# One emission order for the streams of two token mixers

## The chip, the core and the metric

The kernel runs on one core of a Trainium2 chip. The time is device microseconds of one execution. TensorE (PE) multiplies matrices, VectorE (DVE), ScalarE (ACT) and GpSimd (POOL) work element by element, and SyncE (SP) issues nearly all loads. Each of these takes its own instructions in the order in which the built program lists them, and waits on semaphores for the others.

## What is computed

One decoder layer on 256 tokens of width 1,024, in float32: a SwiGLU layer, then two token mixers side by side, then cross-attention to a memory, then a second SwiGLU layer, each with a residual and a layer norm. The change is in the mixers:

```python
g_ssd, g_att, z, xbc, dt_raw, q, c_kv, q_idx, k_idx, w_idx = split_cols(x @ w_in, IN_SPLITS)
y_ssd = ssd_branch(z, xbc, dt_raw, ...)
y_att = dsa_branch(q, c_kv, q_idx, k_idx, w_idx, ...)
merged = sigmoid(g_ssd) * (y_ssd @ w_proj_ssd) + sigmoid(g_att) * (y_att @ w_proj_att)
x = layer_norm(ALPHA * x + merged @ w_out)
```

`ssd_branch` is a state-space mixer: a causal convolution of width 4 over 2,048 channels and a SiLU, then a scan in two chunks of 128 tokens over 16 heads, a gate by `z` and a norm by groups. `dsa_branch` is sparse attention: 16 index heads give each query a score for each key, the 64 best keys stay (top-k), and 16 heads attend to them. The projection of `y_ssd` needs the whole scan. The attention's softmax needs the top-k. The gates `g_ssd` and `g_att` need neither.

## The kernel before

**Weights.** A unit of work is a matrix of 1,024 by 256 weights in two pieces of 512 KB. A piece is loaded by SP into one of 4 `raw` buffers, ACT rounds it into `whi` (line 150), DVE takes the rest into `wlo` (line 151), with 6 buffers each. PE then runs 24 matmuls of 256 columns (line 116): high by high, high by low, low by high for eight blocks of 128 features. A unit asks for a PSUM buffer of the group `mm`, of which there are 4; scores take one of 2 in `s`, transposes and small products one of 2 in `t`. Where a call passes `pool=True`, POOL takes the rest of the second piece instead of DVE.

**Streams.** The mixers are written as generators, and `fly` interleaves them. It keeps a clock of its own, `self.pe`, which counts matmul columns, and each generator yields either a pause on that clock or the name of a mark that it waits for. Of the streams that are due it always resumes the first in the list. What `fly` emits is then scheduled once more by the tile framework, which may set instructions of one engine ahead of others. The order that results is fixed in the program.

**Two groups.** The first `fly` runs `ssd_decay` (softplus and decay, lines 533 to 565), `latent` (the keys' latent, `cT`), `xbc` (the convolution: 8 units, and after each the convolution of its 2 blocks of 128 channels on ACT and DVE, lines 454 to 458) and `k_index`. The second runs `dsa` (index projections `w_qidx`, the scores with sums `acc` on DVE in line 695, the top-k in lines 701 and 702, then `w_q` and the attention heads), `ssd` (the scan: `E` are the decays, `xdt` the scaled inputs, `xtok` the output by token, `yT` the normed output turned for the projection) and `fill_mixers` (keys and values of the first four heads, gate 0 in 4 units of `w_gate`, then, after the mark "yT", 4 units of `w_pssd`, then gate 1). Gate 0 waits for the mark "zs", and the second piece of each of its units goes to POOL. Its buffer is slot 4, which holds `zs` (the gate by `z`) before.

**What runs when.** In the program that results, PE does the 16 pieces of `w_xbc` in a row, then the 8 of `w_qidx` between index scores and the scan, then `w_q`, gate 0, and from there one attention head for about every unit of `w_q`, `w_pssd` and gate 1. The last two pieces of gate 1 stand behind the last head, and `w_patt` follows.

Of the kernel before, what the change touches and what calls it, by code (L numbers as in the profile page):

```python
# [19 lines left out]
F32 = mybir.dt.float32  # L20
# [5 lines left out]
P = 128  # L26
T = 256
# [17 lines left out]
WARM = 4  # L45
HEAD_US = 2.4
TOPK_US = 12.0
SSD_US = (2.0, 6.0, 1.0, 5.0)


class Layer:
# [381 lines left out]
    def xbc(self, xT, xtok, bc):  # L433

        nc, t = self.nc, self.t
        late = []

        def flush(n):
            for b, v in (late.pop(0) for _ in range(min(n, len(late)))):
                tp = self.psum("t")[:, :T].rearrange("p (b c) -> p b c", c=P)  # L440
                for tb in range(NTB):
                    self.transpose(tp[:, tb, :], v[:, tb * P:(tb + 1) * P])
                nc.scalar.copy(xtok[:, :, b * P:(b + 1) * P], tp)
        for u in (4, 5, 6, 7, 0, 1, 2, 3):
            ps = self.psum("mm")
            for _ in self.a_steps(ps, t["w_xbc"][u], xT, u % 2 == 1):
                flush(max(0, len(late) - 2))
                yield 0.0
            for i in range(2):
                b = 2 * u + i  # L450
                src = ps[:, i * T:(i + 1) * T]
                v = self.small([P, T], "wa", bufs=4) if b < 8 else bc[:, b - 8, :]
                cw = self.conv_w[:, b, :]
                nc.scalar.activation(v, src, AF.Identity, bias=self.conv_b[:, b:b + 1], scale=cw[:, 3:4])
                for d in (1, 2, 3):
                    self.last_conv = nc.vector.scalar_tensor_tensor(  # L456
                        v[:, d:], src[:, :T - d], cw[:, 3 - d:4 - d], v[:, d:], op0=ALU.mult, op1=ALU.add)
                self.last_silu = nc.scalar.activation(v, v, AF.Silu)
                if b < 8:
                    late.append((b, v))  # L460
            yield 0.0
        yield "kidx"
        flush(len(late))

    def small_proj(self, xT):

# [17 lines left out]
    def latent(self, cT):  # L484

        nc = self.nc
        for tb, c in enumerate(self.ctok):
            sq = self.small([P, 256], "wa", bufs=4)
            ss = self.small([P, 1], "css", bufs=2)
            nc.scalar.activation(sq, c, AF.Square, accum_out=ss)  # L490
            nc.vector.tensor_scalar_mul(ss, ss, 1.0 / 256.0)
            rs = self.rstd(ss, 1, RMS_EPS)
            nc.vector.tensor_scalar_mul(c, c, rs)
        yield 8.0
        for tb, c in enumerate(self.ctok):
            tp = self.psum("t")[:, :256].rearrange("p (k c) -> p k c", c=P)
            for k in range(2):
                self.transpose(tp[:, k, :], c[:, k * P:(k + 1) * P])
                h, l, w = cT[0][:, k, tb * P:(tb + 1) * P], cT[1][:, k, tb * P:(tb + 1) * P], self.kv_w[:, k:k + 1]
                nc.scalar.activation(h, tp[:, k, :], AF.Copy, scale=w)  # L500
                nc.vector.scalar_tensor_tensor(l, tp[:, k, :], w, h.bitcast(F32), op0=ALU.mult, op1=ALU.subtract)
            yield 3.0

    def k_index(self, kidx):

# [28 lines left out]
    def ssd_decay(self):  # L534
# [24 lines left out]
        for tb in range(NTB):  # L559
            nc.gpsimd.dma_start(scr[tb].rearrange("(h l) -> h l", l=P), csT[:, tb, :])  # L560
            e = self.big((7, 9)[tb], F32, (P, H, P), "E")
            nc.gpsimd.dma_start(e.rearrange("p h l -> p (h l)"), scr[tb].partition_broadcast(P))
            nc.gpsimd.tensor_tensor(e, e, cs[:, tb, :].unsqueeze(2).to_broadcast([P, H, P]), op=ALU.subtract)
            self.E.append(e)

    def ssd(self, zs, xtok, bc, yT):

        nc = self.nc
        cs, E, dt, dskip = self.cs, self.E, self.dtr, self.hv[:, 2 * H:3 * H]
        xdt = self.big(3, F32, (P, NTB, D), "xdt")  # L570
        sx = self.big(8, F32, (P, 2, D), "S0xe")
# [81 lines left out]
    def dsa(self, xT, kidx, cT, oT):  # L653
# [5 lines left out]
        def project(name, u, scale):  # L659

            ps = self.psum("mm")
            yield from self.a_steps(ps, t[name][u], xT)
            v = ps.rearrange("p (a b) -> p a b", b=T)
            q = [self.small([P, 2, T], tag, F32R, bufs) for tag, bufs in (("w2a", 2), ("w2e", 4))]
            for i in range(2):
                a, b = slice(i * HD, (i + 1) * HD), slice((1 - i) * HD, (2 - i) * HD)
                nc.scalar.mul(q[i][a], v[a], scale)
                nc.vector.scalar_tensor_tensor(q[i][b], v[a], scale, q[i][a].bitcast(F32),
                                               op0=ALU.mult, op1=ALU.subtract)
            qs.append(q)  # L670

        def scores(q, hh, kh, kl):
# [6 lines left out]
                self.mm(o, q[:, hh // 2, ts], kl, False, True)  # L679
            return ps[:, :384]  # L680
        qs = []
        yield from project("w_qidx", 0, 1.0)
        for u in range(4):
            if u < 3:
# [89 lines left out]
    def keys_values(self, u, cT):  # L774
# [1 line left out]

        nc = self.nc
        w, = self.weight(self.t["w_ukv"][u])
        s = self.big((11, 6)[u % 2], F32R, name="kv")
        kh = s[:, :1024].rearrange("p (i a b) -> p i a b", i=2, b=T)  # L780
        kl = s[:, 1024:].rearrange("p (i a b) -> p i a b", i=2, b=T)
        v0 = self.small([P, 2, T], "w2c", F32R, 2)
# [19 lines left out]
        self.kv.append((kh, kl, vh, vl, v1))  # L802
        yield 0.0

    def fill_mixers(self, xT, cT, yT, gates):
        nc, t = self.nc, self.t
        yield from self.keys_values(0, cT)
        self.done.add("vk")

        def gate(i, u):  # L810
            ps = self.psum("mm")
            yield from self.a_steps(ps, t["w_gate"][4 * i + u], xT, i == 0)
            nc.scalar.activation(gates[i][:, 2 * u:2 * u + 2, :], ps.rearrange("p (a b) -> p a b", b=T),
                                 AF.Tanh, scale=0.5)
        yield "zs"
        for u in range(4):
            yield from gate(0, u)
        yield "yT"
        for u in range(4):
            ps = self.psum("mm")  # L820
            yield from self.a_steps(ps, t["w_pssd"][u], yT)
            g = gates[0][:, 2 * u:2 * u + 2, :]
            nc.vector.scalar_tensor_tensor(g, g, 1.0, ps.rearrange("p (a b) -> p a b", b=T),
                                           op0=ALU.add, op1=ALU.mult)
        for u in range(4):
            yield from gate(1, u)


    def mem_v(self, memT):
# [87 lines left out]
    def run(self):  # L917
# [35 lines left out]
        kidx = [self.small([P, T], tag, F32R, 1) for tag in ("kidxh", "kidxl")]  # L953
        xtok = self.big(10, F32, (P, NTB, D), "xtok")
        bc = self.big(5, F32, (P, 8, T), "bcT")
        self.fly(self.ssd_decay(), self.latent(cT), self.xbc(xT, xtok, bc), self.k_index(kidx))
        yT = self.pairT(7, 9, "yT")
        oT = self.pairT(3, 10, "oT")
        gates = [self.big((4, 5)[i], F32, (P, KB, T), "gate") for i in range(2)]
        self.fly(self.dsa(xT, kidx, cT, oT), self.ssd(zs, xtok, bc, yT), self.fill_mixers(xT, cT, yT, gates))  # L960
        mT = self.pairT(6, 8, "mT")
        for u in range(4):
            ps = self.a_unit(t["w_patt"][u], oT).rearrange("p (a b) -> p a b", b=T)
            k = slice(2 * u, 2 * u + 2)
# [113 lines left out]
```

## Time and profile before

| | us |
|---|---|
| median of 3 runs | 814.89 |
| lowest, highest | 809.25, 816.68 |
| profiled execution | 814.78 |
| its span | 812.9 |
| PE busy | 789.4 |
| DVE busy | 592.4 |
| ACT busy | 448.4 |
| POOL busy | 68.2 |

The span is the time from the first to the last instruction of one profiled execution. PE's busy time counts a matmul from its start to a modelled end, and neighbours overlap by more than half, so work on PE is better counted by the distance from one start to the next. The granted clock of PE is given in shares of full speed.

### The profile page before, as it was taken

The numbers are of one execution on the slowest core, as the hardware profiler recorded it, in microseconds if no ns is written. First come the engines' busy times: TensorE is split into PE (matmuls) and PEld (weight loads), VectorE is DVE, ScalarE is ACT, GpSimd is POOL, SyncE is SP. The second block draws the span as 40 slices with busy tenths as digits, with TensorE's granted clock in tenths as the row PEclk, the third lists the DMA queues.
The fourth block names the chain that finished last, engine by engine and source line by source line (L and its number), as shares of the span: only waits on it lengthen the run. The fifth ranks groups of instructions, "written<-read, shape, count | busy, mean of one in ns | idle before, by whom it ended". The sixth has DMA issues, their size and how long they took to land.

```text
span 812.9 us, 13145 instructions
## 1 busy us (share of the span) xinstructions
PE 789.4 (97%) x5070; PEld 717.5 (88%) x5070; DVE 592.4 (73%) x960; ACT 448.4 (55%) x782; POOL 68.2 (8%) x69
## 2 busy tenths in 40 slices
PE   8999999999989998989999999999999999999996
PEld 5888888887889997989999998899988988888885
DVE  4868776448588989698889767965659777776445
ACT  5756565433476684477667644544444666565330
POOL 1100000000032451230000000200002000000000
PEclk9999999999999999799999999999999999999999
DMA  7876555553656621236444456574433755555531
GB/s 249 271 267 224 193 182 194 187 200 104 210 189 228 208 74 51 81 108 233 165 150 135 158 175 215 170 276 161 156 120 134 256 191 195 192 184 194 192 105 53
DMA packets 39919, 142.90 MB, mean 176 GB/s; under 512 B 4592, under 2 KB 4896, under 8 KB 39472
## 3 DMA queue, kind: packets, MB, share of 16 engines
q1 hardware_dynamic: 38016, 134.63, 49.4%
q0 software_dynamic: 1840, 7.43, 2.9%
q8 instruction: 40, 0.66, 0.3%
q14 instruction: 23, 0.19, 0.1%
HBM read 140.97 MB, written 1.06 MB: 175 GB/s over the span
## 4 chain that ended last, share of the span: by engine, by line
PE 74%; DVE 11%; issue 8%; ACT 4%; DMA 2%; POOL 1%; SPq 0%; DVEq 0%; ACTq 0%; POOLq 0%
PE ps_mm L116 69%; DVE wlo L151 3%; PE ps_t L116 2%; PE ps_t L120 2%; DMA raw<-in_ffn_in_dram 2%; ACT whi L150 1%; PE ps_s L116 1%; DVE acc L695 1%; DVE acc L702 1%; DVE wa L456 1%; DVE m L701 1%; DMA raw<-in_w_pssd_dram 0%; POOL rstd L289 0%; DVE kv L794 0%; DVE kv L793 0%
## 5 line engine op out<-in xcount | busy, mean ns | idle before, releaser
L151 DVE TENSOR_TENSOR wlo<-raw,whi 128x1024 fp32r<-128x1024 f32 (+2 forms) x245 | 301.0, 1231 | 129.1 <-ACT whi L150 125.1
L150 ACT CAST whi<-raw 128x1024 fp32r<-128x1024 f32 (+2 forms) x253 | 263.2, 1044 | 188.1 <-PE ps_mm L116 124.6
L116 PE MATMUL ps_mm<-x1T,whi 128*128 128x256 f32 x768 | 143.9, 288 | 0.0
L116 PE MATMUL ps_mm<-x0T,whi 128*128 128x512 f32 x352 | 123.7, 400 | 2.9 <-ACT whi L150 2.1
L116 PEld LDWEIGHTS ps_mm<-x1T,whi 128*128 128x128 f32 x768 | 122.3, 195 | 0.0
L116 PE MATMUL ps_mm<-x1T,wlo 128*128 128x256 f32 x384 | 110.2, 287 | 0.0
L116 PE MATMUL ps_mm<-x3T,whi 128*128 128x512 f32 x304 | 105.6, 392 | 0.0
L116 PE MATMUL ps_mm<-x0T,wlo 128*128 128x256 f32 x352 | 97.0, 282 | 0.3 <-DVE wlo L151 0.3
L116 PE MATMUL ps_mm<-x3T,wlo 128*128 128x256 f32 x304 | 85.1, 280 | 0.0
L116 PEld LDWEIGHTS ps_mm<-x0T,whi 128*128 128x128 f32 x352 | 65.8, 188 | 20.6 <-ACT whi L150 3.6
L116 PEld LDWEIGHTS ps_mm<-x1T,wlo 128*128 128x128 f32 x384 | 75.1, 195 | 0.0
L116 PEld LDWEIGHTS ps_mm<-x3T,whi 128*128 128x128 f32 x304 | 56.9, 187 | 12.4
L116 PEld LDWEIGHTS ps_mm<-x0T,wlo 128*128 128x128 f32 x352 | 65.7, 189 | 1.6 <-DVE wlo L151 1.4
L116 PE MATMUL ps_mm<-whi,ah 128*128 128x512 f32 x154 | 60.2, 391 | 0.0
L116 PE MATMUL ps_mm<-wlo,ah 128*128 128x512 f32 x154 | 60.1, 390 | 0.0
L116 PE MATMUL ps_mm<-whi,al 128*128 128x512 f32 x154 | 59.9, 389 | 0.0
L116 PEld LDWEIGHTS ps_mm<-x3T,wlo 128*128 128x128 f32 x304 | 57.5, 189 | 0.0
L289 POOL TENSOR_TENSOR rstd<-rstd,mhalf 128x1 f32<-128x1 f32 (+1 forms) x12 | 11.3, 941 | 537.0 <-DVE rstd L288 537.0
L177 DVE TENSOR_TENSOR wa<-wa,ps_mm 128x256 f32<-128x256 f32 x82 | 34.0, 418 | 30.2 <-ACT wa L176 30.1
L347 ACT ACTIVATE wa<-wa 128x256 f32<-128x256 f32 x41 | 17.1, 417 | 48.1 <-DVE wa L177 48.1
L116 PEld LDWEIGHTS ps_mm<-whi,al 128*128 128x128 f32 x154 | 28.9, 188 | 6.2
L116 PEld LDWEIGHTS ps_mm<-whi,ah 128*128 128x128 f32 x154 | 29.0, 188 | 5.6
(296 smaller groups left out, 1551.5 us busy)
## 6 DMA issues: line engine op xcount, KB each, us to landing
raw<-in_ffn_in_dram SPq DMA_DIRECT2D x87, 512.0 KB, 4.1
raw<-in_ffn_out_dram SPq DMA_DIRECT2D x44, 512.0 KB, 3.5
raw<-in_w_xbc_dram SPq DMA_DIRECT2D x16, 512.0 KB, 4.3
raw<-in_w_gate_dram SPq DMA_DIRECT2D x16, 512.0 KB, 3.4
raw<-in_w_z_dram SPq DMA_DIRECT2D x8, 512.0 KB, 3.6
raw<-in_w_qidx_dram SPq DMA_DIRECT2D x8, 512.0 KB, 3.9
raw<-in_w_q_dram SPq DMA_DIRECT2D x8, 512.0 KB, 3.5
raw<-in_w_pssd_dram SPq DMA_DIRECT2D x8, 512.0 KB, 4.6
```

Source lines behind the costliest of these rows:

```text
L116: self.nc.tensor.matmul(out, a, b, start=start, stop=stop)
L120: self.nc.tensor.transpose(out, in_, self.ident)
L150: self.nc.scalar.copy(hi, src)
L151: (engine or self.nc.vector).tensor_sub(lo, src, hi.bitcast(F32))
L177: self.nc.vector.tensor_add(out, out, ps[:, :T])
L289: self.nc.gpsimd.tensor_tensor(v, v, self.mhalf[:, :n], op=ALU.pow)
L347: nc.scalar.activation(sg, self.join(gate, sg), AF.Silu)
L456: self.last_conv = nc.vector.scalar_tensor_tensor(v[:, d:], src[:, :T - d], cw[:, 3 - d:4 - d], v[:, d:], op0=ALU.mult, op1=ALU.add)
L695: nc.vector.scalar_tensor_tensor(acc[:, s], rl[:, s], self.widx[:, tb, h:h + 1], prev[:, s], op0=ALU.mult, op1=ALU.add)
L701: nc.vector.max(m8, acc[:, s])
L702: nc.vector.match_replace(out=acc[:, s], in_to_replace=m8, in_values=acc[:, s], imm_value=KILL)
```

## The change

All seven streams go into one `fly`. `xbc` now yields a pause of 4.0 after each unit, in which streams behind it in the list are resumed: the index projections and scores, the first keys and values, and gate 0. Marks take the place of the group's end: `ssd` waits for "E" (decays broadcast) and "xtok" (the convolution emitted whole), `fill_mixers` for "cT", `dsa` for "kidx". Gate 0 no longer waits for "zs" and no longer uses POOL, and its buffer is slot 6; odd units of keys and values, and then `mT`, take slot 4. `gate` becomes a method.

```diff
--- before.py
+++ after.py
@@ -45,6 +45,7 @@
 WARM = 4
 HEAD_US = 2.4
 TOPK_US = 12.0
+XBC_US = 4.0
 SSD_US = (2.0, 6.0, 1.0, 5.0)
 
 
@@ -458,9 +459,9 @@
                 self.last_silu = nc.scalar.activation(v, v, AF.Silu)
                 if b < 8:
                     late.append((b, v))
-            yield 0.0
-        yield "kidx"
+            yield XBC_US
         flush(len(late))
+        self.done.add("xtok")
 
     def small_proj(self, xT):
 
@@ -500,6 +501,7 @@
                 nc.scalar.activation(h, tp[:, k, :], AF.Copy, scale=w)
                 nc.vector.scalar_tensor_tensor(l, tp[:, k, :], w, h.bitcast(F32), op0=ALU.mult, op1=ALU.subtract)
             yield 3.0
+        self.done.add("cT")
 
     def k_index(self, kidx):
 
@@ -562,10 +564,13 @@
             nc.gpsimd.dma_start(e.rearrange("p h l -> p (h l)"), scr[tb].partition_broadcast(P))
             nc.gpsimd.tensor_tensor(e, e, cs[:, tb, :].unsqueeze(2).to_broadcast([P, H, P]), op=ALU.subtract)
             self.E.append(e)
+        self.done.add("E")
 
     def ssd(self, zs, xtok, bc, yT):
 
         nc = self.nc
+        yield "E"
+        yield "xtok"
         cs, E, dt, dskip = self.cs, self.E, self.dtr, self.hv[:, 2 * H:3 * H]
         xdt = self.big(3, F32, (P, NTB, D), "xdt")
         sx = self.big(8, F32, (P, 2, D), "S0xe")
@@ -679,6 +684,7 @@
                 self.mm(o, q[:, hh // 2, ts], kl, False, True)
             return ps[:, :384]
         qs = []
+        yield "kidx"
         yield from project("w_qidx", 0, 1.0)
         for u in range(4):
             if u < 3:
@@ -776,7 +782,7 @@
 
         nc = self.nc
         w, = self.weight(self.t["w_ukv"][u])
-        s = self.big((11, 6)[u % 2], F32R, name="kv")
+        s = self.big((11, 4)[u % 2], F32R, name="kv")
         kh = s[:, :1024].rearrange("p (i a b) -> p i a b", i=2, b=T)
         kl = s[:, 1024:].rearrange("p (i a b) -> p i a b", i=2, b=T)
         v0 = self.small([P, 2, T], "w2c", F32R, 2)
@@ -802,28 +808,28 @@
         self.kv.append((kh, kl, vh, vl, v1))
         yield 0.0
 
+    def gate(self, g, i, u, xT):
+
+        ps = self.psum("mm")
+        yield from self.a_steps(ps, self.t["w_gate"][4 * i + u], xT)
+        self.nc.scalar.activation(g[:, 2 * u:2 * u + 2, :], ps.rearrange("p (a b) -> p a b", b=T), AF.Tanh, scale=0.5)
+
     def fill_mixers(self, xT, cT, yT, gates):
-        nc, t = self.nc, self.t
+        t = self.t
+        yield "cT"
         yield from self.keys_values(0, cT)
         self.done.add("vk")
-
-        def gate(i, u):
-            ps = self.psum("mm")
-            yield from self.a_steps(ps, t["w_gate"][4 * i + u], xT, i == 0)
-            nc.scalar.activation(gates[i][:, 2 * u:2 * u + 2, :], ps.rearrange("p (a b) -> p a b", b=T),
-                                 AF.Tanh, scale=0.5)
-        yield "zs"
         for u in range(4):
-            yield from gate(0, u)
+            yield from self.gate(gates[0], 0, u, xT)
         yield "yT"
         for u in range(4):
             ps = self.psum("mm")
             yield from self.a_steps(ps, t["w_pssd"][u], yT)
             g = gates[0][:, 2 * u:2 * u + 2, :]
-            nc.vector.scalar_tensor_tensor(g, g, 1.0, ps.rearrange("p (a b) -> p a b", b=T),
-                                           op0=ALU.add, op1=ALU.mult)
+            self.nc.vector.scalar_tensor_tensor(g, g, 1.0, ps.rearrange("p (a b) -> p a b", b=T),
+                                                op0=ALU.add, op1=ALU.mult)
         for u in range(4):
-            yield from gate(1, u)
+            yield from self.gate(gates[1], 1, u, xT)
 
 
     def mem_v(self, memT):
@@ -953,12 +959,12 @@
         kidx = [self.small([P, T], tag, F32R, 1) for tag in ("kidxh", "kidxl")]
         xtok = self.big(10, F32, (P, NTB, D), "xtok")
         bc = self.big(5, F32, (P, 8, T), "bcT")
-        self.fly(self.ssd_decay(), self.latent(cT), self.xbc(xT, xtok, bc), self.k_index(kidx))
         yT = self.pairT(7, 9, "yT")
         oT = self.pairT(3, 10, "oT")
-        gates = [self.big((4, 5)[i], F32, (P, KB, T), "gate") for i in range(2)]
-        self.fly(self.dsa(xT, kidx, cT, oT), self.ssd(zs, xtok, bc, yT), self.fill_mixers(xT, cT, yT, gates))
-        mT = self.pairT(6, 8, "mT")
+        gates = [self.big((6, 5)[i], F32, (P, KB, T), "gate") for i in range(2)]
+        self.fly(self.ssd_decay(), self.latent(cT), self.xbc(xT, xtok, bc), self.k_index(kidx),
+                 self.ssd(zs, xtok, bc, yT), self.dsa(xT, kidx, cT, oT), self.fill_mixers(xT, cT, yT, gates))
+        mT = self.pairT(4, 8, "mT")
         for u in range(4):
             ps = self.a_unit(t["w_patt"][u], oT).rearrange("p (a b) -> p a b", b=T)
             k = slice(2 * u, 2 * u + 2)
```

The program as built holds the same matmuls in another order, and 4 splits of 1,024 columns that were POOL's are DVE's. SP's queue has the same loads. Where 16 loads of `w_xbc` stood in a row before, there now stand 2 of `w_xbc`, 2 of `w_qidx`, 2, 2, 2, then `w_ukv`, 2 of `w_gate`, and so on in turns, and after the last of `w_xbc` come 2 of `w_gate`, 2 of `w_q` and 6 of `w_pssd`. On PE the 16 pieces of `w_xbc` now have 7 pieces of `w_qidx`, 6 of gate 0 and `w_ukv` among them.

PE around the end of the first unit of `w_q`, whose pieces are `x1T,whi` and `x1T,wlo` here. Before, the matmuls behind the transposes of `xtok` (the scan's first chunk) are those of gate 0:

```order
L116 MATMUL ps_mm_3432<-x1T_1390,whi_3440 128x256 x2
L116 MATMUL ps_mm_3432<-x1T_1390,wlo_3441 128x256
L120 MATMUL ps_t_3499<-ident,xtok_2096 128x128 x4
L120 MATMUL ps_t_3512<-ident,xtok_2096 128x128 x4
L116 MATMUL ps_mm_3551<-x1T_1390,whi_3553 128x256 x2
L116 MATMUL ps_mm_3551<-x1T_1390,wlo_3554 128x256
```

PE at the same place in the changed program, where `kv` marks attention scores and `yTh` the projection `w_pssd`:

```order
L117 MATMUL ps_mm_3633<-x1T_1390,whi_3641 128x256 x2
L117 MATMUL ps_mm_3633<-x1T_1390,wlo_3642 128x256
L121 MATMUL ps_t_3747<-ident,xtok_2096 128x128 x4
L121 MATMUL ps_t_3760<-ident,xtok_2096 128x128 x4
L117 MATMUL ps_s_3922<-kv_2546,w2a_3741 128x256 x4
L117 MATMUL ps_s_3976<-kv_2546,w2e_3742 128x256 x4
L117 MATMUL ps_s_4093<-kv_2546,w2a_3741 128x256 x4
L121 MATMUL ps_t_3773<-ident,xtok_2096 128x128 x4
L117 MATMUL ps_mm_3799<-yTh_2098,whi_3801 128x256
L117 MATMUL ps_mm_3861<-yTh_2098,whi_3863 128x256
L117 MATMUL ps_mm_3939<-yTh_2098,whi_3941 128x256
L121 MATMUL ps_t_3786<-ident,xtok_2096 128x128 x4
```

Behind the same transposes there are now three attention scores, which need the two buffers of `s`, then the transposes of the second chunk, then `w_pssd`; the units of gate 0 have moved ahead.

DVE where the top-k begins. Before, the second chunk's sum by `w2d` and its product with `zs` stand ahead of the first `MAX`:

```order
L632 TENSOR_TENSOR xtok_2096<-xtok_2096,w2d_3337 128x512
L695 SCALAR_TENSOR_TENSOR acc_2791<-wa_3345,widx_2003,acc_2791 128x128
L634 TENSOR_TENSOR xtok_2096<-xtok_2096,zs_1849 128x1024
L151 TENSOR_TENSOR wlo_3616<-raw_3614,whi_3615 128x1024
L151 TENSOR_TENSOR wlo_3694<-raw_3692,whi_3693 128x1024
L695 SCALAR_TENSOR_TENSOR acc_2791<-wa_3369,widx_2003,acc_2791 128x256
L695 SCALAR_TENSOR_TENSOR acc_2791<-wa_3369,widx_2003,acc_2791 128x128
L695 SCALAR_TENSOR_TENSOR acc_2791<-wa_3378,widx_2003,acc_2791 128x256
L695 SCALAR_TENSOR_TENSOR acc_2791<-wa_3378,widx_2003,acc_2791 128x128
L701 MAX m_579_3382<-acc_2791 128x8
```

DVE in the changed program, from the last step of the top-k on:

```order
L707 MAX m_613_3628<-acc_2222 128x8
L708 MATCH_REPLACE acc_2222<-m_612_3625,acc_2222 128x256
L708 MATCH_REPLACE acc_2222<-m_613_3628,acc_2222 128x128
L637 TENSOR_TENSOR xtok_2096<-xtok_2096,w2d_3683 128x512
L709 TENSOR_SCALAR acc_2222<-acc_2222 128x384
L628 TENSOR_TENSOR xtok_2096<-xtok_2096,ps_mm_3686 128x512
L710 TENSOR_TENSOR acc_2222<-acc_2222,dist 128x384
L635 TENSOR_TENSOR w2d_3699<-ps_mm_3696,ecs_3413 128x512
L673 SCALAR_TENSOR_TENSOR w2a_3741<-ps_mm_3633,w2a_3741 64x512
L637 TENSOR_TENSOR xtok_2096<-xtok_2096,w2d_3699 128x512
L232 SCALAR_TENSOR_TENSOR yTl_2099<-ps_t_3747,feat,yTh_2098 128x128
L639 TENSOR_TENSOR xtok_2096<-xtok_2096,zs_1849 128x1024
```

The second chunk's sums and its product with `zs` now stand behind the top-k.

PE at the end of the attention. Before, the last head's values (`kidxl` is the buffer of the last third of them) are followed by two pieces of gate 1:

```order
L116 MATMUL ps_mm_5044<-wb_5053,w2c_4640 128x256
L116 MATMUL ps_mm_5044<-w2d_5054,w2c_4640 128x256
L116 MATMUL ps_mm_5044<-wb_5053,w2c_4640 128x256
L116 MATMUL ps_mm_5044<-wc_5055,kidxl_4641 128x128
L116 MATMUL ps_mm_5092<-x1T_1390,whi_5094 128x256 x2
L116 MATMUL ps_mm_5092<-x1T_1390,wlo_5095 128x256
```

PE in the changed program, from the last matmul of gate 1's last piece on (`x1T,wlo` in its first row):

```order
L117 MATMUL ps_mm_4844<-x1T_1390,wlo_4853 128x256
L117 MATMUL ps_mm_4927<-wb_4936,w2c_4521 128x256
L117 MATMUL ps_mm_4927<-w2d_4937,w2c_4521 128x256
L117 MATMUL ps_mm_4927<-wb_4936,w2c_4521 128x256
L117 MATMUL ps_mm_4927<-wc_4938,kidxh_4522 128x128
L121 MATMUL ps_t_4990<-ident,wa_4832 128x128 x3
L117 MATMUL ps_s_5000<-kv_4887,w2a_4803 128x256 x4
L117 MATMUL ps_s_5032<-kv_4887,w2e_4804 128x256 x4
L117 MATMUL ps_mm_5017<-wb_4994,w2c_4521 128x256
L117 MATMUL ps_s_5066<-kv_4887,w2a_4803 128x256 x4
L121 MATMUL ps_t_5022<-ident,wa_4947 128x128 x3
```

The last pieces of gate 1 have moved ahead of the last heads: behind them now stand the values of 7 heads, the transposes of 6 and the scores of 4, with 14 matmuls of `w_patt` ahead of the last head's transposes.

## Rows read from the trace of the kernel before

**Rows 1.** The page, part 1: busy us (share of the span) and instructions of the engines

```profile
PE 789.4 (97%) x5070; PEld 717.5 (88%) x5070; DVE 592.4 (73%) x960; ACT 448.4 (55%) x782; POOL 68.2 (8%) x69
```

**Rows 2.** Busy time by stretch: the three stretches of the token mixers

```profile
core 0: us, PE busy (x) PEld busy (x) DVE busy (x) ACT busy (x) POOL busy (x), PEclk, DMA share, GB/s
227.00:280.50 53.50, 49.61 (x402) 49.14 (x401) 47.09 (x84) 33.77 (x60) 21.51 (x11) 0.97 0.63 215
280.50:370.40 89.90, 83.75 (x632) 81.88 (x631) 78.02 (x165) 56.20 (x116) 23.97 (x11) 0.92 0.26 84
370.40:469.30 98.90, 97.52 (x811) 96.47 (x810) 86.00 (x174) 69.33 (x166) 2.29 (x4) 1.00 0.51 171
```

**Rows 3.** Timeline of PE, several stretches: start us, us, line, operation, tiles, count

```profile
243.91 0.48 PE L120 MATMUL ps_t<-ident,wb 128*128 128x128 f32 x1 [3.10 <-DVE cTl L501]
...
321.88 1.90 PE L116 MATMUL ps_mm<-xdt,E 128*128 128x64 f32 x16
...
325.31 6.69 PE L116 MATMUL ps_mm<-xdt,E 128*128 128x64 f32 x32 [1.02 <-ACT S0xe L613]
...
338.58 0.28 PE L116 MATMUL ps_s<-kidxh,w2a 128*128 128x256 f32 x1
...
338.70 0.28 PE L116 MATMUL ps_s<-kidxl,w2a 128*128 128x256 f32 x1
```

**Rows 4.** Busy time by stretch, five microseconds in the scan

```profile
330.00:335.00 5.00, 5.00 (x22) 4.64 (x21) 2.51 (x4) 0.78 (x3) 0.00 (x0) 0.50 0.26 97
```

**Rows 5.** Timeline of DVE, several stretches: start us, us of the group, count last

```profile
254.82 1.51 DVE L456 SCALAR_TENSOR_TENSOR bcT<-ps_mm,feat,bcT 128x255 f32<-128x255 f32 x3
...
320.97 2.34 DVE L151 TENSOR_TENSOR wlo<-raw,whi 128x1024 fp32r<-128x1024 f32 x2
...
332.72 1.22 DVE L634 TENSOR_TENSOR xtok<-xtok,zs 128x1024 f32<-128x1024 f32 x1
...
337.04 0.69 DVE L623 TENSOR_TENSOR xtok<-xtok,ps_mm 128x512 f32<-128x512 f32 x1 [2.49 <-PE ps_mm L116]
...
347.02 1.40 DVE L695 SCALAR_TENSOR_TENSOR acc<-wa,widx,acc 128x256 f32<-128x256 f32 x4
...
348.34 0.41 DVE L701 MAX8 m<-acc 128x8 f32<-128x256 f32 x1
...
357.69 0.27 DVE L702 MATCH_REPLACE8 acc<-m,acc 128x128 f32<-128x128 f32 x1
...
360.55 0.61 DVE L231 SCALAR_TENSOR_TENSOR yTl<-ps_t,feat,yTh 128x128 fp32r<-128x128 f32 x2
...
377.92 0.61 DVE L721 TENSOR_REDUCE amax<-wa 128x1 f32<-128x256 f32 x2
...
381.92 0.54 DVE L726 TENSOR_SCALAR wa<-wa,asum 128x256 f32<-128x256 f32 x2
...
384.22 0.41 DVE L151 TENSOR_TENSOR w2d<-ps_t,wb 128x256 fp32r<-128x256 f32 x1
...
384.55 0.55 DVE L718 SCALAR_TENSOR_TENSOR wa<-acc,ps_s 128x384 f32<-128x384 f32 x1
```

**Rows 6.** Busy time by stretch: DVE from the last convolution to the last yT

```profile
288.50:371.00 82.50, 71.66 (x155) 0.92 0.24 78
```

**Rows 7.** Timeline of DVE and then of POOL, where both work at once

```profile
272.19 3.21 DVE L151 TENSOR_TENSOR wlo<-raw,whi 128x1024 fp32r<-128x1024 f32 x1
...
296.75 3.73 DVE L695 SCALAR_TENSOR_TENSOR acc<-wa,widx,caus 128x256 f32<-128x256 f32 x2
...
269.73 4.59 POOL L563 TENSOR_TENSOR E<-E,cs 128x2048 f32<-128x2048 f32 x1
...
291.76 4.67 POOL L580 TENSOR_TENSOR xdt<-xtok,dtr 128x1024 f32<-128x1024 f32 x2 [17.43 <-ACT xtok L443]
...
298.25 4.00 POOL L584 TENSOR_TENSOR xtok<-xtok,hv 128x1024 f32<-128x1024 f32 x2
```

**Rows 8.** ACT, view of one source line: count, ns min/median/max, first to last start

```profile
L801 ACT COPY kidxh<-ps_mm x2: 354/364/373, 339.9 to 410.6; 128x256 f32<-128x256 f32 x2
```


## The prediction

> **What bounds the kernel now.** I read the page first, then the busy time by stretch, then PE's timeline, then DVE's and POOL's. The page gives PE 97% of the span [rows 1], so a change can win only where PE stands idle or runs at half clock, or lose by making more of that. All that moves lies between the first matmul of `w_xbc` at 227.0 and the first of `w_patt` at 469.3, 242.3 us. The three stretches there [rows 2] show where PE loses: 3.9 us idle in the convolution, 6.1 us idle and a clock of 0.92 in the stretch of the index scores, the scan, the top-k and gate 0, and only 1.4 us beside the attention. DVE is 88%, 87% and 87% busy in the three, so it is nearly a second bound. In the scan PE was left waiting and fell to a granted clock of 0.50, the 1.2 GHz level [rows 4]: 16 products of `xdt` and `E` take 1.90 us at full clock, but the group of 32 is spread over 6.69 us [rows 3].
>
> PE's matmuls are the same before and after, so I add up how long each piece of the new order lasts and set that against 242.3. The price of a matmul of 256 columns is the distance of two starts, 338.58 to 338.70, so 0.12 us [rows 3], and a piece of weights (24 of them) takes 2.88 us.
>
> **First piece, up to the last matmul of `w_xbc`.** The program puts 16 pieces of `w_xbc`, 7 of `w_qidx`, 6 of gate 0, `w_ukv` (24 matmuls) and the scores of 8 index heads (4 each) here: 752 matmuls, 90.2 us, with some 12 transposes and two small products, 92 us. DVE has 42 convolution steps at 0.50, 30 splits at 1.17, 16 sums at 0.35, some 11 instructions at 0.69 or less [rows 5], and what the convolution's stretch now holds beside its own steps and splits, some 9 us of decay and latent work: 78 us, so PE sets the pace. What it may lose: nothing at the least, and at the most what the convolution's stretch loses now, 53.5 less 47.4 of matmuls, 6.1. Most of that is one wait of 3.10 us for `cTl` [rows 3], which is still met, since five or six splits, as now, stand ahead of `cTl` in DVE's order. I take 4, in the middle, because DVE's share falls from 88% to 81%: **96 us**. The four splits that POOL loses cost DVE 4.7 us here, hidden under PE; if PE were not the bound, they would count in full. The loads of this piece are 30 times 0.5 MB in 96 us, 164 GB/s, less than the 215 GB/s of the convolution now [rows 2], so I cost SP's new order at nothing. The other slots cost nothing: `zs` is read for the last time long before the second `w_ukv` writes slot 4.
>
> **Second piece, until `w_pssd` runs in full.** This is where I expect the change to pay back what it saves. Gate 0 used to stand behind the scan; it kept PE busy during the top-k and while DVE turned `yT`. Now it has been used up, and `w_pssd` needs `yT`. DVE's order sets the length. From the last two blocks of the convolution to the last split of `yT` it holds, at the prices of [rows 5]: 6 convolution steps (3.0), 5 splits (5.9), 14 instructions over 512 columns at 0.69 (9.7), 8 over 1,024 or 2,048 columns at 1.22 (9.8, `E` priced like the product with `zs`), 16 index sums (5.6), the top-k from 348.34 to 357.96 and two short passes behind it (10.6), 16 splits of `yT` at 0.30 (4.9), and the start of the first attention heads (2.9): 52 us. That is the lower end, DVE without a pause. For the upper end I take the present way from the last convolution to the last `yT`, in which DVE is busy 71.66 of 82.50 us, 87% [rows 6]: 52 over 0.87 is 60. I take **58**, near the upper end, because what made DVE pause is still there: POOL takes 10.5 us for `xdt` and what follows from it [rows 7], ACT makes the exponentials, and PE answers at half clock after a wait. In addition the second chunk's sums now stand behind the top-k instead of ahead of it, and the norm, the transposes and `yT` of that chunk follow one after another. PE's own work there is 5 pieces (14.4), 8 index heads (3.8), 12 attention scores (1.4), 32 products at 0.12 (3.8), about 8 us of the other scan products and transposes, and the first 25 matmuls of `w_pssd` (3.0): 35 us. So PE stands some 23 us in this piece.
>
> **Third piece, to the last matmul of gate 1.** 25 pieces of weights less the 25 matmuls already done make 69 us, and some ten heads of attention 12 more: 81. The loss is at least the 1.4 us of the present stretch beside the attention [rows 2], at most the 6.1 above. I take 3, since DVE's share there is as it was: **84**.
>
> **Fourth piece, the last heads.** The filler is used up while several heads are still open, and at the end DVE alone sets the pace. Four heads cost it 0.55 for the scores, 0.61 and 0.54 for maxima and scaling and 0.1 for the reciprocal [rows 5], 7.2 us; the end of a fifth 0.6; 14 splits of 256 columns at 0.41 make 5.7; a split of `w_patt` 1.2. That is 14.7, and 2.3 us of PE and ACT ahead of the first and behind the last: 17 us, of which 21 matmuls of `w_patt` use 2.5. Net **14.5**; 10.5 if DVE has a quarter of it done ahead, 17 if it pauses as in the second piece.
>
> The sum is 96 + 58 + 84 + 14.5 = 252.5 us in place of 242.3, 10.2 more. Against the profiled execution of 814.8 us, 0.1 under the median, this gives **825 us**. With all the low ends it is 92 + 52 + 82.4 + 10.5, 809; with the high ends 98 + 60 + 87 + 17, 834.
>
> **Rivals.** *The pauses pay (815 us).* With two other streams to turn to, PE loses nothing in the first piece (92), it stays at full clock, DVE then never waits for it in the scan (53), and the rest comes to 83 and 14: 242 us, as now. For it speaks that DVE's largest single wait in the scan, 2.49 us, was for such slow products of PE [rows 3, 5]; against it that POOL's and ACT's steps are no faster. It decides if `w_pssd` runs in full within 144 us of the first `w_xbc`; I expect 154.
>
> *POOL holds DVE up (832 us).* A split that takes 1.17 us took 3.21 when it met POOL's work on `E`, and ended 1.1 us after it (272.19 + 3.21 = 275.40; 269.73 + 4.59 = 274.32) [rows 7]. In the scan five POOL instructions run from 291.76 to 302.25, 10.5 us, and two index sums took 3.73 instead of 0.70, 3.0 us lost. Now the products on `E` and the sums of the last five index heads fall into these 10.5 us. If DVE stands through all of them, it loses 7.5 us more than now. The Trainium skill, in "SBUF — State Buffer", section "Who interferes with whom", says that a VectorE instruction with two SBUF inputs and a GpSimd instruction that reads SBUF exclude each other for a whole instruction. By that rule this rival is the rule's full price; the trace agrees on the single split and bears out a third of the price in the scan.
>
> *A PSUM buffer is held (832 us).* The last third of `w_ukv` is copied into the index keys' buffer, so it waits for the last index score: now at 339.9 [rows 8], some 40 us after its matmuls. In the new order it holds one of the 4 `mm` buffers from the middle of the first piece to the scan. If PE then waits 1.5 us for DVE's convolution in each of the last five units, that is 7.5 us.
>
> That the change does not do what it says I leave out: the new program's order shows the moved pieces.
>
> **Chances.** My forecast 0.50, the pauses 0.26, the two slow rivals 0.16 together, and 0.08 for a gain that none of these rows shows. About 1%, 8 us, is what a measurement tells from no change, so the border to slower is 823. Of my forecast two thirds (0.34) lie above it, with the slow rivals 0.50. The rest of it (0.16) and most of the pauses (0.20) make 0.36 for no change. The lower edge of the pauses (0.06) and the unexplained gain make 0.14 for faster. The range reaches from 810, the sum of all low ends, to 838, the slow rivals with some of the high ends.
>
> **What the new profile would show.** The last `w_xbc` matmul at about 323 with little idle time before it; if it is later than 327, a held buffer or DVE is to blame. Then a stretch of some 55 us in which PE is about 60% busy and its clock falls, with waits for `yTl` and for the top-k's successors. Then a full PE until gate 1 ends near 465, and some 15 us of heads without filler. If PE is never idle for over 5 us between 323 and 381, my second step is wrong; if `w_patt` starts in full before 470, the sum is.

## The result, and the profile after

The changed kernel takes 837.3 us (835.24 to 838.02) against 814.79, a ratio of 1.0284 (95% interval 1.0231 to 1.0337): 22.5 us slower, where 10.2 were forecast. Its profiled execution took 837.71 us. One of the ten executions of the kernel with gate 0 cut in two, below, took 1286 us at a granted clock of 0.56; the ratios leave such slow executions out. The page of the changed kernel, part 1, which answers to [rows 1]:

```profile
PE 794.4 (95%) x5070; PEld 720.5 (86%) x5070; DVE 599.4 (72%) x964; ACT 449.6 (54%) x782; POOL 56.7 (7%) x65
```

PE's share fell from 97% to 95%; its work is the same. Busy time of the changed kernel in three stretches: the prediction's first piece, its second, and the rest up to 501.04, where three of the eight pieces of `w_patt` are done; the last row is a part of the first (columns as in [rows 2]):

```profile
core 0: us, PE busy (x) PEld busy (x) DVE busy (x) ACT busy (x) POOL busy (x), PEclk, DMA share, GB/s
227.13:332.07 104.94, 96.60 (x773) 96.01 (x773) 79.52 (x128) 59.78 (x99) 19.67 (x11) 0.95 0.54 181
332.07:393.40 61.33, 44.88 (x312) 42.02 (x312) 57.99 (x130) 35.29 (x84) 14.60 (x7) 0.83 0.18 60
393.40:501.04 107.64, 103.42 (x830) 100.89 (x829) 84.58 (x172) 69.18 (x163) 2.29 (x4) 0.98 0.41 135
274.37:279.72 5.35, 5.35 (x26) 5.35 (x27) 5.29 (x8) 0.45 (x2) 0.00 (x0) 0.53 0.18 51
```

In the first piece the clock is 0.95, and PE is busy 96.6 of 104.9 us; in the piece of weights from 274.37 to 279.72 the clock is 0.53. In the second DVE is busy 58.0 of 61.3 us (95%), while PE is busy 44.9 at a clock of 0.83. PE's timeline in the changed kernel, as in [rows 3]; the bracket is the idle time ahead of the row and what ended it:

```profile
268.14 0.28 PE L117 MATMUL ps_s<-kidxl,w2e 128*128 128x256 f32 x1
274.37 0.77 PE L117 MATMUL ps_mm<-x1T,whi 128*128 128x256 f32 x2 [5.95 <-DVE bcT L457]
...
346.20 0.28 PE L117 MATMUL ps_s<-kidxl,w2e 128*128 128x256 f32 x1
350.06 1.13 PE L117 MATMUL ps_mm<-S0xe,w2c 128*128 128x256 f32 x4 [3.58 <-POOL S0xe L587]
...
379.59 1.23 PE L117 MATMUL ps_s<-kv,w2a 128*128 128x256 f32 x4 [8.41 <-DVE w2a L673]
```

PE's two large waits are 5.95 us in the convolution, ahead of the piece `w_xbc.6`, for a step of DVE on `bcT`, and 8.41 us ahead of the attention's scores, for DVE behind the top-k. The 3.58 us ahead of `S0xe` wait for POOL. Up to the last `w_xbc` matmul the only other wait over 0.8 us is one of 2.17 for `cTl`. DVE's timeline in the changed kernel at the first of these waits, where [rows 7] had two slow rows:

```profile
262.62 0.48 DVE L457 SCALAR_TENSOR_TENSOR bcT<-ps_mm,feat,bcT 128x255 f32<-128x255 f32 x1 [2.16 <-ACT bcT L455]
263.01 3.43 DVE L701 SCALAR_TENSOR_TENSOR acc<-wa,widx,caus 128x256 f32<-128x256 f32 x1
266.37 0.47 DVE L457 SCALAR_TENSOR_TENSOR bcT<-ps_mm,feat,bcT 128x254 f32<-128x254 f32 x1
266.76 2.08 DVE L701 SCALAR_TENSOR_TENSOR acc<-wa,widx,caus 128x128 f32<-128x128 f32 x1
...
270.96 1.63 DVE L701 SCALAR_TENSOR_TENSOR acc<-wa,widx,acc 128x256 f32<-128x256 f32 x1
```

An index sum over 256 columns takes 3.43 us, one over 128 columns 2.08, while the convolution steps between them keep their 0.47. In the scan of the same kernel (DVE's timeline):

```profile
344.93 3.32 DVE L701 SCALAR_TENSOR_TENSOR acc<-wa,widx,acc 128x256 f32<-128x256 f32 x2
...
348.77 9.13 DVE L611 TENSOR_TENSOR E<-E,w2b 128x1024 f32<-128x1024 f32 x4
```

Two sums take 3.32 us and the four products of `E` and `w2b` 9.13. POOL's timeline of the changed kernel, as in [rows 7]:

```profile
262.56 3.61 POOL L565 TENSOR_TENSOR E<-E,cs 128x2048 f32<-128x2048 f32 x1 [5.89 <-DMA E<-cs_rows]
266.14 2.56 POOL L152 TENSOR_TENSOR wlo<-raw,whi 128x1024 fp32r<-128x1024 f32 x1
268.66 3.65 POOL L565 TENSOR_TENSOR E<-E,cs 128x2048 f32<-128x2048 f32 x1
...
343.15 4.95 POOL L585 TENSOR_TENSOR xdt<-xtok,dtr 128x1024 f32<-128x1024 f32 x2 [23.31 <-ACT xtok L444]
348.06 1.94 POOL L587 TENSOR_TENSOR S0xe<-xdt,dte 128x1024 f32<-128x1024 f32 x1
349.97 5.72 POOL L589 TENSOR_TENSOR xtok<-xtok,hv 128x1024 f32<-128x1024 f32 x2
```

POOL works on `E` (with one split between) from 262.56 to 272.3 and on the scan's inputs from 343.15 to 355.7, and in just those stretches DVE's rows are long. The first and third of the long sums stand beside a subtraction on `E`, the second (266.76) beside the split between the two. So far that is a coincidence in time.

### The profile page after: what moved, and what is told of

It reads as the page before. It is cut to its first block, busy times and chain, and to the rows that moved or that the text cites. A ratio compares the mean times of both kernels' runs of the same rounds, so it can differ in the third digit from the quotient of the medians.

```text
span 836.0 us, 13153 instructions
## 1 busy us (share of the span) xinstructions
PE 794.4 (95%) x5070; PEld 720.5 (86%) x5070; DVE 599.4 (72%) x964; ACT 449.6 (54%) x782; POOL 56.7 (7%) x65
## 4 chain that ended last, share of the span: by engine, by line
PE 49%; DVE 3%; ACT 1%; issue 0%; DVEq 0%; ACTq 0%
PE ps_mm L117 44%; PE ps_t L117 2%; PE ps_t L121 1%; PE ps_s L117 1%; DVE wlo L152 0%; DVE amax L727 0%; ACT whi L151 0%; DVE wa L724 0%; DVE kv L800 0%; DVE oTl L152 0%; DVE kv L799 0%; ACT kv L798 0%; DVE w2d L152 0%; ACT kv L797 0%; DVE wa L732 0%
## 5 line engine op out<-in xcount | busy, mean ns | idle before, releaser
L117 PE MATMUL ps_mm<-x0T,wlo 128*128 128x256 f32 x352 | 96.8, 281 | 0.3 <-DVE wlo L152 0.3
```

Of the source, the lines that this page charges most:

```text
L117: self.nc.tensor.matmul(out, a, b, start=start, stop=stop)
```

## The experiments

**E's subtractions left out.** Theory A: POOL's instructions hold DVE, and so PE. Theory B: the PSUM buffer that `w_ukv`'s last third holds makes PE wait.

```diff
-            nc.gpsimd.tensor_tensor(e, e, cs[:, tb, :].unsqueeze(2)..., op=ALU.subtract)
```

> The changed kernel without POOL's two subtractions on E (3.6 us each), which leaves that part of the decays out; nothing of DVE, PE or ACT goes. Theory A, POOL holds DVE up: the index sums that took 3.43, 2.08 and 1.63 us at 263 to 272.6 fall back to 0.48 and 0.35, PE's wait of 5.95 us ahead of w_xbc.6 goes, and with it the half clock behind it (2.3 us), so the last w_xbc matmul comes near 324 instead of 332.1 and the time is 829. Theory B, the held PSUM buffer alone: DVE's work of the unit before is what PE waits for with one buffer too few, POOL or not, so at least 4 of the 5.95 us stay and the time is 835 or more.

829.25 us, ratio 1.0186 (1.0138 to 1.0234): 8.0 less than the changed kernel. DVE's timeline, the same three sums:

```profile
264.13 0.48 DVE L700 SCALAR_TENSOR_TENSOR acc<-wa,widx,caus 128x256 f32<-128x256 f32 x1
...
264.92 0.34 DVE L700 SCALAR_TENSOR_TENSOR acc<-wa,widx,caus 128x128 f32<-128x128 f32 x1
...
266.97 0.48 DVE L700 SCALAR_TENSOR_TENSOR acc<-wa,widx,acc 128x256 f32<-128x256 f32 x1
```

They take 0.48, 0.34 and 0.48 us, and the wait of 5.95 us is gone. POOL's split, which had stood behind the first subtraction, now runs at 259.64, before the sums. Busy time up to the last `w_xbc` matmul:

```profile
227.62:324.40 96.78, 94.32 (x773) 93.73 (x773) 73.67 (x128) 59.74 (x99) 12.31 (x9) 0.98 0.58 197
```

The first piece is 96.8 us instead of 104.9, which is the 96 that the prediction had. The rest of the kernel kept its length. Theory A holds for the convolution. Theory B alone is out: the last third of `w_ukv` is copied out only at 351.4 here and at 359.1 in the changed kernel, so the buffer is held through all of this piece in both, and without POOL's work PE has no wait over 0.8 us in it but the 2.17.

**The copy that holds the buffer left out.**

```diff
-        v1 = self.small([P, T], ("kidxh", "kidxl")[u % 2], bufs=1)
+        v1 = self.small([P, T], ("kidxh", "kidxl")[u % 2], bufs=1) if u else self.x[:, 0, :T]
...
-        nc.scalar.copy(v1, ps[:, 1, :])
+        if u > 0:
+            nc.scalar.copy(v1, ps[:, 1, :])
...
```

> The changed kernel in which the last third of the first w_ukv is not copied out (one ACT copy left out, the values of heads 0 to 3 read another tile), so that its PSUM buffer comes free with the split beside it instead of with the last index score. POOL's work stays. Theory B, the held buffer: with four buffers instead of three PE can run w_xbc.6 and w_xbc.7 (5.8 us) while DVE is late, the wait of 5.95 us goes or falls under 1 us, last w_xbc near 324, time 829. Theory A, POOL's hold on DVE alone: DVE has still lost its 6 us, the wait only moves to the next unit that needs DVE's splits or buffers; time 835 to 838.

835.81 us, ratio 1.0267 (1.022 to 1.0314). DVE's timeline still has a long sum, beside the subtraction in POOL's, and PE's the wait behind it:

```profile
264.87 3.73 DVE L701 SCALAR_TENSOR_TENSOR acc<-wa,widx,caus 128x128 f32<-128x128 f32 x1
...
274.84 0.42 DVE L152 TENSOR_TENSOR w2c<-ps_mm,w2c 128x256 fp32r<-128x256 f32 x1
```

```profile
264.84 3.61 POOL L565 TENSOR_TENSOR E<-E,cs 128x2048 f32<-128x2048 f32 x1 [7.11 <-DMA E<-cs_rows]
```

```profile
273.18 0.47 PE L117 MATMUL ps_mm<-x1T,whi 128*128 128x256 f32 x2 [3.69 <-DVE bcT L457]
```

The wait shrinks from 5.95 to 3.69 us and the time by 1.5, as theory A has it. That is not the buffer's doing: the split of `w2c` at 274.84, which now frees the buffer, stands behind the held sums in DVE's order and comes after PE's wait has ended. What changed is that POOL waited 7.11 us for `E` instead of 5.89, so the sums lost 4.1 us (3.73 and 1.01 less 0.34 twice) instead of 5.8. So this run does not tell what a buffer free in time would have hidden; that the held buffer is not enough by itself, the run before shows.

**Gate 0 late, and the index late.** Theory C: the filler (work of PE that waits for nothing, here gate 0) is used up too early. Rival D: the index sums in the convolution are what costs. The first kernel puts gate 0 back behind the scan, the second the index work.

```diff
         self.done.add("vk")
+        yield "zs"
         for u in range(4):
```

> The changed kernel, but gate 0 waits for the mark zs again as before the change (without POOL); the index scores stay in the pauses of the convolution. Theory C, the filler is used up too early: gate 0 now stands beside the top-k and yT, so the second piece loses most of its 23 us of idle time on PE, and gate 1 stands behind the last head, so no head goes without filler; w_patt starts some 15 us earlier than in the changed kernel and the time is 815 to 822, whatever the convolution loses. Rival D, the index scores in the convolution are what costs: PE has less other work there, DVE the same, so the convolution's stretch loses as much as the changed kernel's and the time stays at 830 or more.

829.57 us, ratio 1.0192 (1.0152 to 1.0232): far from C's 815 to 822 and 0.4 under D's 830. Up to the last `w_xbc` matmul PE has only two waits over 0.8 us, 2.17 and 2.23, so D's reason is wrong. C had missed the scan. With the top-k drawn ahead of it and gate 0 behind it, PE has nothing there. Busy time in two stretches from 323 to 360 us, then PE's timeline:

```profile
323.00:340.00 17.00, 7.33 (x34) 5.46 (x33) 17.00 (x61) 9.15 (x16) 9.35 (x5) 0.69 0.02 6
340.00:360.00 20.00, 19.93 (x111) 19.23 (x110) 13.24 (x18) 4.00 (x13) 1.95 (x1) 0.66 0.05 15
```

```profile
331.14 3.78 PE L117 MATMUL ps_mm<-S0xe,w2c 128*128 128x256 f32 x8 [3.65 <-POOL S0xe L587]
339.55 10.50 PE L117 MATMUL ps_mm<-xdt,E 128*128 128x64 f32 x48 [4.62 <-DVE E L611]
```

PE is busy 7.33 of 17 us, and then runs at a clock of 0.66 for 20 us. The hole had only moved.

```diff
-        yield "kidx"
+        yield "xtok"
         yield from project("w_qidx", 0, 1.0)
```

> The changed kernel, but the index projections wait for the mark xtok, so that only gate 0 and the first keys and values run in the pauses of the convolution. Theory C: still more heads stand behind the last filler (all 16 come after gate 1, with 6 pieces of w_q and three w_ukv as PE's only other work: 45 us of PE beside some 58 us of DVE), so 13 us or more are lost there and the time is 840 to 855. Rival D: with no index sums in the convolution the wait of 5.95 us ahead of w_xbc.6 is gone, as is any over 3 us there, and the time falls to 825 or less.

842.97 us, ratio 1.0359 (1.0317 to 1.0402), in C's range. The wait of 5.95 us is gone, as D has it, but the time rises. All heads stand behind gate 1 now. Busy time from 330 to 390, and from the end of gate 1 to where three pieces of `w_patt` are done:

```profile
330.00:390.00 60.00, 55.24 (x356) 54.33 (x357) 37.73 (x69) 27.73 (x65) 2.06 (x2) 0.76 0.27 85
429.12:506.37 77.25, 66.91 (x481) 61.28 (x480) 69.17 (x167) 53.60 (x149) 2.28 (x4) 0.96 0.35 112
```

In the second row DVE is busy 69.2 of 77.3 us (90%) and so seems to set the pace, and PE is idle 10.3. But that is less than half of the 28 us over the kernel before: the first row, the scan and the start of `w_pssd`, has a clock of 0.76, which C had not named.

**The scan's products on DVE.**

```diff
-            nc.gpsimd.tensor_tensor(hview(xdt[:, tb, :]), hview(xtok[:, tb, :]), ...)
+            nc.vector.tensor_tensor(hview(xdt[:, tb, :]), hview(xtok[:, tb, :]), ...)
```

and so for `S0xe` and `xtok` (lines 587 and 589).

> The changed kernel with the scan's five products on xdt, S0xe and xtok on DVE instead of POOL (five instructions over 1,024 columns at 1.2 us, 6.1 us more for DVE); POOL keeps the two subtractions on E in the convolution. Theory A, POOL's instructions hold DVE for their own length: the four products on E in the scan fall from 9.13 back to 4.6 us and the two index sums at 344.9 from 3.32 to 0.75, 7.1 us back for 6.1 given, and the wait of 3.58 us for S0xe shortens; w_pssd runs in full 59 to 63 us after the last w_xbc matmul (61.4 before) and the time is 833 to 838. Rival, those products were slow for another reason: they stay slow, DVE has 6 us more, and the time is 842 or more.

841.45 us, ratio 1.0295 (1.0248 to 1.0343). DVE's timeline in the scan, then busy time in two stretches of it:

```profile
344.24 2.36 DVE L585 TENSOR_TENSOR xdt<-xtok,dtr 128x1024 f32<-128x1024 f32 x2
...
351.65 0.75 DVE L701 SCALAR_TENSOR_TENSOR acc<-wa,widx,acc 128x256 f32<-128x256 f32 x2
...
353.07 4.63 DVE L611 TENSOR_TENSOR E<-E,w2b 128x1024 f32<-128x1024 f32 x4
```

```profile
346.00:356.00 10.00, 6.87 (x48) 5.76 (x48) 9.93 (x12) 7.22 (x12) 0.00 (x0) 1.00 0.11 41
356.00:366.00 10.00, 10.00 (x62) 10.00 (x61) 6.27 (x14) 1.81 (x3) 0.00 (x0) 0.66 0.00 0
```

The four products take 4.63 us and the two sums 0.75, as theory A says: 7.1 us come back. The time is still near the rival's end (842 or more), not in theory A's 833 to 838. The five products cost DVE 5.9 us (two of them 2.36), PE is idle 2.96 us behind them and then falls to a clock of 0.66, and DVE, busy 6.27 of 10 us there, waits for it in turn. POOL holding DVE is real in the scan too; giving DVE the work is no cure.

**Gate 0 cut in two.**

```diff
-        for u in range(4):
-            yield from self.gate(gates[0], 0, u, xT)
+        yield "xtok"
+        yield from self.gate(gates[0], 0, 0, xT)
+        yield from self.gate(gates[0], 0, 1, xT)
+        yield "zs"
+        yield from self.gate(gates[0], 0, 2, xT)
+        yield from self.gate(gates[0], 0, 3, xT)
```

> The changed kernel with gate 0 cut in two: units 0 and 1 wait for the mark xtok, units 2 and 3 for zs, so that four pieces stand in the scan and four behind it; the index scores stay in the convolution. Theory C, the filler decides: in the kernel with gate 0 whole behind zs PE stood 9.4 us in the scan and ran at half clock from 327 to 355 (48 products of xdt and E took 10.5 us instead of some 5.7); four pieces there end both, 12 to 15 us less than its 829.6, so 814 to 818. Rival E, DVE sets the scan's pace (it was 100% busy from 320 to 340 there): the four pieces bring four splits of 1.2 us to DVE and hide nothing it would not have waited for; 826 to 834.

815.97 us, ratio 1.001 (0.998 to 1.004): 13.6 less than with gate 0 behind the scan, as C has it, and all of the change's loss is gone; rival E's 826 to 834 is out. DVE's timeline shows that POOL still holds it near 270:

```profile
270.48 5.42 DVE L701 SCALAR_TENSOR_TENSOR acc<-wa,widx,acc 128x256 f32<-128x256 f32 x2
```

Two sums take 5.42 us, but here they stand behind the convolution steps and `kv` in DVE's order, and PE has no wait near them. What a hold costs depends on what is queued behind the held instruction.

**The same with E's subtractions on DVE.**

```diff
-            nc.gpsimd.tensor_tensor(e, e, cs[:, tb, :].unsqueeze(2)..., op=ALU.subtract)
+            nc.vector.tensor_tensor(e, e, cs[:, tb, :].unsqueeze(2)..., op=ALU.subtract)
```

> As the kernel with gate 0 cut in two, and the two subtractions on E on DVE instead of POOL (2.4 us each). Theory A: POOL then has no work beside the index sums, DVE gives 4.8 us and gets back 5 to 6, PE's wait near 289 (2.2 us, and half clock behind it) goes: 2 to 4 us under the kernel with gate 0 cut in two, 811 to 815 by theory C. Rival: DVE's share in the convolution is near 90%, so its 4.8 us more show on PE: 3 to 5 us over that kernel.

822.32 us, ratio 1.0086 (1.0054 to 1.0118): 6.3 slower, so my expectation failed; the rival has the direction, but neither its size (3 to 5) nor its reason. DVE's timeline, then PE's:

```profile
268.81 2.29 DVE L565 TENSOR_TENSOR E<-E,cs 128x2048 f32<-128x2048 f32 x1 [7.52 <-DMA E<-cs_rows]
...
272.32 2.28 DVE L565 TENSOR_TENSOR E<-E,cs 128x2048 f32<-128x2048 f32 x1
```

```profile
278.64 0.77 PE L117 MATMUL ps_mm<-x1T,whi 128*128 128x256 f32 x2 [6.91 <-DVE bcT L457]
```

DVE itself stood 7.52 us for the broadcast of `E`, since the subtraction stands in its order; on POOL that wait hurt nobody. The convolution step is late behind it, and PE waits 6.91 us.

**Three quarters of gate 0 in the scan.** Units 0 to 2 wait for `xtok`, the last for `zs`; first with E's subtractions on DVE, then on POOL.

> As the kernel before it (gate 0 cut, E on DVE), but three units of gate 0 wait for xtok and only the last for zs. Theory C: PE's waits for the softmax and for yT behind the top-k are then covered by two pieces instead of four; if that cover was needed, some 3 to 6 us slower than the cut in halves. Rival: the scan needs the cover more than the heads do, and it is 1 to 4 us faster.

816.78 us, ratio 1.0006 (0.9979 to 1.0034), 5.5 less than the halves with `E` on DVE, where I expected 3 to 6 more: the rival has the direction, and the scan needs the cover more.

> The changed kernel with three units of gate 0 behind the mark xtok and the last behind zs, and the subtractions on E on POOL as in the changed kernel. Theory C: all of gate 0's eight pieces then lie where the scan and the top-k leave PE without work. With E on DVE this order gave 816.8 and the cut in halves 822.3; with E on POOL the halves gave 816.0, 6.3 less; so 816.8 less 6.3, 808 to 813. Rival: POOL's subtractions hold the index sums here as in the changed kernel and cost PE 5 us or more near 268; 815 to 819.

810.18 us, ratio 0.996 (0.9932 to 0.9988). That is the fastest order, 0.4% under the kernel before: a small gain, under the 1% that was set as the border. POOL's subtractions hold two sums here too (5.02 us from 268.41), but PE has no wait over 0.8 us between 241 and 287, so the rival is out. Busy time of its three stretches, cut as those of the changed kernel above:

```profile
226.66:312.30 85.64, 81.67 (x670) 81.24 (x669) 74.19 (x129) 55.59 (x96) 19.98 (x11) 0.98 0.55 192
312.30:382.40 70.10, 66.33 (x533) 64.01 (x533) 63.55 (x157) 49.46 (x119) 13.93 (x8) 1.00 0.24 79
382.40:472.70 90.30, 87.14 (x715) 86.31 (x714) 74.99 (x147) 58.88 (x131) 1.61 (x3) 0.98 0.53 173
```

PE is busy 66.3 of 70.1 us in the second piece, at a clock of 1.00. POOL's timeline and DVE's in that scan:

```profile
323.15 3.77 POOL L585 TENSOR_TENSOR xdt<-xtok,dtr 128x1024 f32<-128x1024 f32 x2 [28.71 <-ACT xtok L444]
326.87 1.91 POOL L587 TENSOR_TENSOR S0xe<-xdt,dte 128x1024 f32<-128x1024 f32 x1
328.73 3.77 POOL L589 TENSOR_TENSOR xtok<-xtok,hv 128x1024 f32<-128x1024 f32 x2
```

```profile
324.42 0.61 DVE L707 MAX8 m<-acc 128x8 f32<-128x256 f32 x2
...
325.00 0.41 DVE L708 MATCH_REPLACE8 acc<-m,acc 128x256 f32<-128x256 f32 x1
...
335.98 4.62 DVE L611 TENSOR_TENSOR E<-E,w2b 128x1024 f32<-128x1024 f32 x4
```

DVE does the top-k while POOL does its five products, and neither is slowed: pairs of POOL's take 3.77 us, where they took 4.95 and 5.72 beside the sums and products, and the four products on `E` are back at 4.62.

**The latent later.** One number, in the kernel just told and in the kernel before.

```diff
-        yield 8.0
+        yield 11.0
```

> As the kernel before it, and the latent's transposes wait 11 instead of 8 on the emission clock. PE's wait of 2.17 us near 239 (the first transpose of wb behind cTl) goes, and with it 1.6 us of half clock behind it: 3 to 4 us less than the kernel before it, 805 to 809. Rival: ACT's and DVE's order, not the transpose's place, sets that wait, and it only moves: within 1.5 us of the kernel before it.

810.09 us, ratio 0.9958 (0.9936 to 0.998): the wait began at 243.42 instead of 238.65 and is 2.27 us long. The rival holds.

> The kernel before the change with the latent's transposes 11 instead of 8 later, nothing else. PE's wait of 3.10 us near 241 and the half clock behind it (1.7 us) go or move: 810 to 813 if they go, 814 to 816 if they move. This tells what part of the kernel above comes from the new order and what from the latent alone.

812.76 us, ratio 0.998 (0.9954 to 1.0006): no difference that can be measured. The wait moved here too (2.83 us ahead of 248.69, 3.10 before), so the time says nothing of what its going would be worth.

## Why the prediction was right and wrong

The direction was right, and so were the places: the last two pieces came close to the forecast. From `w_pssd` in full to the last matmul of gate 1 (476.4) it took 83.0 us, forecast 84; the last heads took 16.0 net, forecast 14.5. The size was wrong, and the first piece is the step that failed. That 837.3 lies within 810 to 838 is luck in part: the upper end came from POOL's hold in the scan and a held buffer, and most of the excess is a hold in the convolution. (The sum of all low ends is 809, as the prediction first has it, not 810.)

- **First piece: 96 forecast, 104.9 measured.** The term of 4 us for losses was 12.9. The 6.1 taken as its upper end came from a stretch in which POOL held a split of DVE (3.21 us in [rows 7]) and PE had no wait over 0.8 us behind it. I had seen that hold, and the new order puts index sums into the convolution, where the subtractions on `E` run, but I put the rival "POOL holds DVE up" into the scan alone. In the convolution it cost 8.1 us, shown by leaving the subtractions out. The sums lost 5.8 us (3.43, 2.08 and 1.63 less 0.48, 0.34 and 0.48), PE waited 5.95, and the piece behind the wait ran at half clock, 5.35 us instead of 3.04. Of the two that the prediction would blame for a last `w_xbc` matmul later than 327 (it came at 332.07), it was DVE.
- **Second piece: 58 forecast, 61.3 measured.** My count for DVE was 52, and it was busy 58.0: the products on `E` lost 4.5 us to POOL (9.13 less 4.62) and two sums 2.6. The pauses were 3.3 us, not 6. PE stood some 16 us (61.33 less 44.88), not 23.
- **"DVE's share falls to 81%, so PE sets the pace."** The share was 76% (79.5 of 104.9), and PE waited for DVE all the same. A share over the whole piece says nothing of 10 us in which DVE is held.
- **"A PSUM buffer is held."** It was held, from the first piece to 359.1, but the five waits of 1.5 us did not come: behind the one of 5.95 us PE has none over 0.8 in the rest of the piece, and without POOL's subtractions none in the whole piece but that for `cTl`. What a free buffer would have hidden of the 5.95 us, no run shows.
- **"The pauses pay."** `w_pssd` ran in full 166 us after the first `w_xbc`, so this rival is out; but with gate 0 kept for the scan its price, 815, is met or passed (816.0 and 810.2). The loss was not in one order for all streams; it was in spending gate 0 (6 of its 8 pieces) in the convolution, which had no need of it. Moving gate 0 alone gives back the convolution's 8 us as well, since DVE's order there changes with it.

The sum by pieces is 104.9 + 61.3 + 83.0 + 16.0 = 265.2 for 242.3 before, 22.9 more, as is the difference between the two profiled executions.

The Trainium skill, "SBUF — State Buffer", section "Who interferes with whom", which the prediction cites beside the rival on POOL, says that DVE instructions with two SBUF inputs are those that a reading GpSimd instruction excludes. The trace agrees: index sums and products are held, the convolution steps, with one input in PSUM, are not (0.47 us between two held sums).

Not settled: how much of the second piece's 3.3 us over the forecast is POOL's doing. Taking POOL's products away there gave DVE work of the same size, so no run parts the two.

## What to carry to other kernels

When instructions are moved, look at what the other engine runs at their new place: two that never met before may now exclude each other, and the price is what is left of the other's instruction (3.4 us of 3.6 here), for all that is queued behind the held one. Filler is worth most where the order has a hole, so before spending it name the stretch that has no work of its own, and leave it some; here three quarters of gate 0 kept for the scan gave 810.2, three quarters of it (6 of its 8 pieces) in the convolution 837.3. An instruction that waits for a transfer is best put on an engine with nothing urgent behind it: on DVE the wait for `E` cost 6.3 us here.

## What the runs showed of the hardware

- A sum of 0.34 us took 3.73 in the run with the copy left out: it began at 264.87, 0.03 us after a POOL instruction of 3.61 us, and ended 0.15 us after that did. It was held until POOL's instruction ended, not slowed by some ratio.
- The maxima and replacements of the top-k ran beside POOL at 0.61 us for a pair and 0.41 for one (324.42 and 325.00 above), as they do in the changed kernel while POOL stands still (0.61 at 370.34 and 0.40 at 370.93), and POOL's products took 3.77 us a pair there.
